# Dilated keys in a stage of their own: Strassen's seven block products, two projection units at a time, and rotations that exchange halves by transfers

## The chip, the cores and the metric

The kernel runs on one core of one Trainium2 chip. The metric is the device time of one execution in microseconds; lower is better. The kernel before takes 1445.66 us (median of 3 runs, 1445.48 to 1445.92).

Engines are named as the profile names them: PE is TensorE's matmul stream and PEld its weight loads, DVE is VectorE, ACT ScalarE, POOL GpSimd, SP the engine whose queue issues most transfers.

## What is computed

An encoder block on x of 1024 tokens x 1024 channels. `h = rms_norm(x)` is projected by `w_in` to the inputs of three parallel mixers and their gates. This case is about the first mixer, dilated window attention with 3 groups of 8 heads (head size 64), at windows and dilations (128, 1), (512, 4), (2048, 16):

```python
aq = rope(a_qkv[:, :, 0], pos)
ak = rope(a_qkv[:, :, 1], pos)
av = a_qkv[:, :, 2]
for gi, (window, dil) in enumerate(A_GROUPS):
    o_g, lse_g = dilated_window_attention(aq[:, :, hs], ak[:, :, hs], av[:, :, hs], window, dil)
oa = sum over the groups, weighted by softmax of their log-denominators

def rope(x, pos):                      # per head: x1, x2 are its halves of 32
    return concat([x1 * cos - x2 * sin, x1 * sin + x2 * cos])
```

The other mixers are global attention with axial rotary positions and attention into a fixed memory of 256 tokens. Each mixer is gated by SiLU, projected, merged by sigmoid gates and projected again; a normalised sum with x is the output.

## The kernel before, in words

All is computed in float32 precision by three float32r passes: each operand is split into a high part (ACT copy, L105) and a low part (DVE subtraction, L106), and each product is high x high + high x low + low x high. `h` (up to its row factors) stays in SBUF all the time as `hh` and `hl`, 8 tiles of 128 channels x 1024 tokens each.

A **unit** is 128 output channels of a projection: two halves of 512 tokens, 24 matmuls of 128x512 each (`dense`, L139 on; L143, L145 and L147 are its three passes), in two PSUM banks `d`. Each half is evacuated by the unit's own function. Units stand in `queue`; `prepare` loads and splits a unit's weights one unit ahead (buffers `wr`, two, and `wh`/`wl`, two each). PE's order is written out by hand: `weave` runs the dense matmuls of some units and a list of attention pieces in parallel, each piece having a declared cost, so that both progress in proportion. In some stages DVE, ACT, POOL and SP follow the written order too (`manual_schedule`); elsewhere the scheduler orders them.

The stages that matter, by time in the profile:

- The **value stage** (461.8 to 581.4 us, L836 to L1012, all engines in written order) makes the values of the three dilation groups. One group is made in the classical way (16 steps of 12 matmuls, `v_first`), then the other two together by Strassen's seven block products of 512 x 512 (`PRODUCTS`, L844; 28 steps of 12 matmuls). The operands S1 to S4 are sums of weight blocks (`sum_at`, on POOL, L902), T1 to T4 sums of token blocks, made earlier and kept in DRAM as `tsd`. `split_at` splits operands two steps ahead, `blocks_at` loads token blocks five steps ahead. `v_evac` combines products on DVE, `v_store` scales on ACT and stores to DRAM (`vdr`). Between the steps, `operand` rescales the global mixer's output (L942, L943) in eight pieces, one every 4 steps, through single buffers `vot`, `vgt`, `vrt`. The rotation tables `tab` are loaded and scaled here as well.
- The **dilated stage** (581.4 to 1007.9 us, L1018 to L1410) works on 12 items: 4 head pairs x 3 groups. An item needs its query and its key unit, rotated. `rope_half` (L1040) does it for half a unit: four 32-partition DVE multiplications with the sine that read the other half of the head from PSUM, one of 128 partitions with the cosine, and an addition on POOL (L1056), which also regroups tokens by residue class. Three units run before the first scores (`weave(3)`, L1387, written order), then two units beside each item's attention. The pieces of an item (`plan`, L1242): scores of four query tiles at a time (L1137), `soft` per tile (DVE minimum L1149, ACT exponential L1150), transposes of a tile two tiles later (L1167 or L1176, copied out by ACT, L1179, from one of two banks `tr`), and twice an item the products with the values (L1193, copied out by ACT, L1201). Values are loaded for each item between its two score blocks (L1081 on). After every third item the groups are combined (`combine`, L1297). In the last two items four gate units run in place of queries and keys.
- The **closing gate stage** (1007.9 to 1219.6 us) makes 22 gate units in 11 pairs by the same seven products, one product being 12 matmuls into one bank. Its token blocks T1 to T3 are loaded during the last item into buffers that are free by then.

Of the kernel before, what the change touches and what calls it, by code (L numbers as in the profile page):

```python
# [15 lines left out]
S = 1024  # L16
NT = 8
P = 128
# [32 lines left out]
def block(ctx: ExitStack, tc: tile.TileContext, x, xT, memT, cst, msk, bcst, tabA, gpost,  # L51
# [181 lines left out]
    vdr = dram.tile([3, 4, S, 128], F32, name="vdr")  # L233

# [410 lines left out]
    def first_values():  # L645

        hl_ = []
        for i in range(2):
            raw = wp.tile([P, 1024], F32, name="wr", bufs=WR)
            nc.sync.dma_start(raw.rearrange("p (k f) -> p k f", k=2), wv[VG[0], :, 2 * i:2 * i + 2])  # L650
# [186 lines left out]
    v_first = ready.pop(len(queue))  # L837
# [3 lines left out]
    tbp, tb = pool("tb")  # L841
    tab = [tb.tile([P, S], F32, name=f"tab{j}") for j in range(2)]
    vpp, vp = pool("vp")
    PRODUCTS = (("A11", "B11"), ("A12", "B21"), ("S2", "T2"), ("S3", "T3"), ("S4", "B22"), ("S1", "T1"), ("A22", "T4"))  # L844
# [7 lines left out]
    slots0 = [slot() for _ in range(4)]  # L852
    def rs():
        return vp.tile([P, 512], F32, name="vr", bufs=5)

    raw1 = vp.tile([P, 4, 512], F32, name="sum1")
    for i in range(2):
        nc.sync.dma_start(raw1[:, 2 * i:2 * i + 2], wv[VG[0], :, 4 + 2 * i:6 + 2 * i])
    VR = {}
    for nm, u, kh in (("A21", 1, 0), ("A11", 0, 0), ("A22", 1, 1), ("A12", 0, 1)):  # L860
        VR[nm] = vp.tile([P, 4, 512], F32, name=f"v{nm}")
        for i in range(2):
            nc.sync.dma_start(VR[nm][:, 2 * i:2 * i + 2], wv[VG[1 + u], :, 4 * kh + 2 * i:4 * kh + 2 * i + 2])
    VR.update(S1=raw1, S3=VR["A21"], S2=VR["A11"], S4=VR["A12"])
    vv = [vp.tile([P, 512], F32, name=f"vv{j}") for j in range(4)]
    vy = [vp.tile([P, 512], F32, name=f"vy{j}") for j in range(4)]
    SB, TB_ = {}, {}
# [13 lines left out]
    def split_at(i, k):  # L881
        an, bn = PRODUCTS[i]
# [25 lines left out]

    def v_out(u, t, j, ps_, z):
        r = rs()  # L910
# [21 lines left out]
    def operand(r, stage):  # L932
        k, t = r // 2, half[r % 2]
        if stage == 0:
            OT[r] = [vp.tile([P, 512], F32, name=x) for x in ("vot", "vgt", "vrt")]
# [17 lines left out]
    FIRST = 16  # L953
    steps_v = [(None, e, k) for e in range(2) for k in range(8)] + [(i, 0, k) for i in range(7) for k in range(4)]
    left = []
    for n, (i, e, k) in enumerate(steps_v):
        if k == 0:
            now = v_banks()
        for j in range(4):
            if i is None:  # L960
                t = slice(e * 512 + j * 128, e * 512 + j * 128 + 128)
                (bh, bl), w, end = (hh[k][:, t], hl[k][:, t]), v_first[k], 7
# [6 lines left out]
        if n + 2 < 8 and n + 2 >= 4:  # L969
            v_first.append(slots0[n - 2])  # L970
            split(*parts_of(v_first[-1]), raw1[:, n - 2])
        m = n + 2 - FIRST
        if 0 <= m < 28:
            split_at(*divmod(m, 4))
        for f in behind:
            f()
        m = n + 5 - FIRST
        if 0 <= m < 28:
# [8 lines left out]
        if n == FIRST + 10:  # L987
            for j in range(2):
                nc.sync.dma_start(tab[j], tabA[:, j])
        if n == FIRST + 17:  # L990
            V.tensor_tensor(tab[0], tab[0], rb, op=OP.mult)
            G.tensor_tensor(tab[1], tab[1], rb, op=OP.mult)
        if n == FIRST + 16:
            early[len(queue)] = lambda: [wp.tile([P, 1024], F32, name="wr", bufs=WR)]
            prepare(len(queue))
            nc.sync.dma_start(ready[len(queue)][0], wu[0])
        if n == FIRST + 25:
            raw = ready.pop(len(queue))[0]
            w = wslot(0), wslot(1)
            split(*w, raw)  # L1000
            ready[len(queue)] = tuple(z.rearrange("p (k f) -> p k f", k=8) for z in w)
        if k == end:
            for j in range(4):
                if i is None:
                    left.append(lambda b=now[j], T=4 * e + j: [lambda: v_store(rs(), VG[0], T, b)])
                else:
                    left.append(lambda i=i, j=j, b=now[j]: v_evac(i, j, b))
    for f in left:
        for g in f():
            g()  # L1010
    manual.__exit__(None, None, None)
    close(vpp)  # L1012
# [7 lines left out]
    with tc.tile_pool(name="aa", bufs=1, reuse_waits="tile") as aa:  # L1020
# [19 lines left out]
        def rope_half(o, half, p, scale, g):  # L1040

            t = slice(half * 512, half * 512 + 512)
            t1 = ab.tile([P, 512], F32, name="t1a", bufs=3)
            t2 = ab.tile([P, 512], F32, name="t2a", bufs=3)
            cos, sin = tab[0][:, t], tab[1][:, t]

            def mult(out, x, y):
                if scale is None:
                    return V.tensor_tensor(out, x, y, op=OP.mult)  # L1049
                return V.scalar_tensor_tensor(out, x, scale, y, op0=OP.mult, op1=OP.mult)  # L1050
# [5 lines left out]
            G.tensor_tensor(half_of(o, half, g), classes(t1, g), classes(t2, g), op=OP.add)  # L1056

        def add_a(p_, g):
            base = (p_ * 3 + g) * 2
# [803 lines left out]
```

## Time and profile before

| | |
|---|---|
| median of 3 runs | 1445.66 us |
| the profiled execution | 1445.34 us |
| span of its trace | 1443.5 us |
| PE, PEld busy | 1420.8, 1142.4 us |
| DVE, ACT, POOL busy | 979.8, 631.7, 499.7 us |
| transfers | 168.26 MB, mean 117 GB/s |
| TensorE clock granted | 0.999 |

The page splits the span by engine and gives the chain of work that ended last. A busy PE is not PE at its peak: a matmul of 128x512 is shown 389 ns long, while the next may start sooner, so what counts is the distance between starts. A row of the windows table holds, for each engine, its busy time in that stretch and the number of instructions.

### The profile page before, as it was taken

To read this page: it belongs to the slowest core of one execution; us is meant where nothing else is said; L and a number is where in the kernel's file an instruction comes from. 1 tells how busy PE (TensorE), PEld (TensorE's weight loads), DVE (VectorE), ACT (ScalarE), POOL (GpSimd) and SP (SyncE) were. 2 spreads that over 40 slices of the span, in tenths; PEclk is the share of its full clock that TensorE was granted. 3 is DMA by queue.
4 is the path that set the end of the run, shared out by engine and by line. 5 is a ranking of instruction groups with operands and counts; after the bars stand their busy time and mean duration, and the time that the engine had idled before them with its cause. 6 is when DMAs were issued, how large, how long until landed. Compare 5 with 4: busy or idle time off the path is not lost.

```text
span 1443.5 us, 20974 instructions
## 1 busy us (share of the span) xinstructions
PE 1420.8 (98%) x7628; PEld 1142.4 (79%) x7628; DVE 979.8 (68%) x1723; ACT 631.7 (44%) x1361; POOL 499.7 (35%) x382
## 2 busy tenths in 40 slices
PE   7999999999999999999999999999999999999998
PEld 7899986566666888888788888778887888888887
DVE  7765468776772267775697686864778778559643
ACT  6544355665654253244444534554443434223231
POOL 1415504666674421232233241321333331044322
PEclk9999999999999999999999999999999999999999
DMA  6332012232111775511132142343444453757122
GB/s 238 104 117 74 16 66 92 81 97 83 55 52 40 249 226 181 152 48 43 47 94 76 53 105 54 99 129 88 141 147 139 175 175 116 285 205 286 41 89 102
DMA packets 99448, 168.26 MB, mean 117 GB/s; under 512 B 21968, under 2 KB 51728, under 8 KB 99344
## 3 DMA queue, kind: packets, MB, share of 16 engines
q1 hardware_dynamic: 80192, 148.95, 32.1%
q10 hardware_dynamic: 19152, 17.96, 3.7%
q8 instruction: 60, 0.98, 0.3%
q14 instruction: 44, 0.36, 0.1%
HBM read 124.57 MB, written 42.30 MB: 116 GB/s over the span
## 4 chain that ended last, share of the span: by engine, by line
PE 76%; DVE 12%; ACT 4%; issue 4%; POOL 3%; DMA 1%; ACTq 0%; SPq 0%; POOLq 0%; DVEq 0%
PE sc L125 9%; PE s L125 8%; PE d L145 8%; PE d L143 8%; PE d L147 8%; PE s L967 6%; PE sc L1709 5%; PE ov L754 3%; PE tr L1193 2%; PE d L967 2%; PE s L738 2%; PE tr L720 2%; PE s L739 2%; PE d L535 2%; PE s L1137 2%
## 5 line engine op out<-in xcount | busy, mean ns | idle before, releaser
L143 PE MATMUL d<-hh,wh 128*128 128x512 f32 x672 | 270.2, 402 | 2.2 <-DVE fth L222 1.7
L145 PE MATMUL d<-hl,wh 128*128 128x512 f32 x672 | 268.0, 399 | 0.0
L147 PE MATMUL d<-hh,wl 128*128 128x512 f32 x672 | 267.9, 399 | 0.0
L105 ACT ACTIVATE wh<-wr 128x1024 fp32r<-128x1024 f32 (+1 forms) x79 | 72.2, 916 | 212.0 <-PE d L145 116.7
L143 PEld LDWEIGHTS d<-hh,wh 128*128 128x128 f32 x672 | 126.5, 188 | 32.6 <-issue 3.9
L145 PEld LDWEIGHTS d<-hl,wh 128*128 128x128 f32 x672 | 126.6, 188 | 29.9 <-issue 6.6
L745 POOL TENSOR_TENSOR bl<-bl,bp 128x512 f32<-128x512 f32 x96 | 131.4, 1369 | 53.7 <-ACT bp L741 48.2
L147 PEld LDWEIGHTS d<-hh,wl 128*128 128x128 f32 x672 | 126.5, 188 | 28.5 <-issue 4.5
L125 PE MATMUL sc<-hh,wh 128*128 128x512 f32 x384 | 118.5, 389 | 0.0
L1056 POOL TENSOR_TENSOR aq<-t1a,t2a 128x512 f32<-128x512 f32 x24 | 45.5, 1897 | 171.2 <-DVE t1a L1050 157.1
L1150 ACT ACTIVATE pra<-pra,sts 128x192 f32<-128x192 f32 (+2 forms) x192 | 84.2, 440 | 32.5 <-DVE sts L1149 32.4
L721 DVE TENSOR_REDUCE bn<-tr 128x1 f32<-128x512 f32 x128 | 86.0, 685 | 17.4 <-PE tr L720 16.1
L741 ACT ACTIVATE bp<-s 128x512 f32<-128x512 f32 x128 | 75.8, 595 | 46.7 <-PE s L739 45.8
L106 DVE TENSOR_TENSOR wl<-wr,wh 128x1024 fp32r<-128x1024 f32 x53 | 73.6, 1390 | 31.9 <-ACT wh L105 31.5
L1050 DVE SCALAR_TENSOR_TENSOR t2a<-d,tab 32x512 f32<-32x512 f32 x96 | 66.0, 687 | 38.3 <-PE d L147 36.7
L1056 POOL TENSOR_TENSOR ak<-t1a,t2a 128x512 f32<-128x512 f32 x24 | 55.1, 2294 | 103.8 <-DVE t1a L1049 103.8
L1049 DVE TENSOR_TENSOR t2a<-d,tab 32x512 f32<-32x512 f32 x96 | 66.0, 687 | 34.6 <-PE d L147 33.2
L125 PEld LDWEIGHTS sc<-hh,wh 128*128 128x128 f32 x384 | 72.1, 188 | 14.9
L1436 POOL TENSOR_TENSOR sf<-wr 128x512 f32<-128x512 f32 x22 | 31.0, 1427 | 146.2 <-DMA wr<-in_wu 60.5
L1640 POOL TENSOR_TENSOR acc<-acc,th 128x1024 f32<-128x1024 f32 x15 | 40.9, 2727 | 110.1 <-DVE th L1639 110.1
L125 PE MATMUL sc<-hl,wh 128*128 128x512 f32 x192 | 74.7, 389 | 0.0
L1149 DVE CUSTOM_DVE_ANT_0 pra<-s,mask 128x192 f32<-128x192 f32 (+2 forms) x192 | 55.9, 347 | 17.3 <-PE s L1137 15.5
(369 smaller groups left out, 3396.2 us busy)
## 6 DMA issues: line engine op xcount, KB each, us to landing
wr<-in_wu SPq DMA_DIRECT2D x64, 512.0 KB
th<-thd SPq DMA_DIRECT2D x24, 512.0 KB
thd<-rs ACTq DMA_DIRECT2D x44, 256.0 KB
g2d<-fth SPq DMA_DIRECT2D x24, 256.0 KB
vdr<-vr ACTq DMA_DIRECT2D x24, 256.0 KB
wgt<-wgd SPq DMA_DIRECT2D x24, 256.0 KB
ot<-od SPq DMA_DIRECT2D x12, 512.0 KB
wr<-in_wbr SPq DMA_DIRECT2D x24, 256.0 KB
```

The costliest lines, as they stand in the source:

```text
L105: A.activation(dst_h, src, AF.Copy)
L106: V.tensor_tensor(dst_l, src, dst_h.bitcast(F32), op=OP.subtract)
L125: PE.matmul(out_ps, a, b, start=i == 0, stop=i == n - 1)
L143: PE.matmul(dst, wh[:, k, :], hh[k][:, t], start=k == 0, stop=False)
L145: PE.matmul(dst, wh[:, k, :], hl[k][:, t], start=False, stop=False)
L147: PE.matmul(dst, wl[:, k, :], hh[k][:, t], start=False, stop=k == 7)
L721: fp["last"] = V.tensor_reduce(st[i]["n"][:, j, c:c + 1], s, axis=AX.X, op=OP.min)
L741: A.activation(pp, s, AF.Exp, scale=-1.0)
L745: G.tensor_tensor(lsum[i % 2], lsum[i % 2], pp, op=OP.add)
L967: PE.matmul(now[j], a, b, start=k == 0 and q == 0, stop=k == end and q == 2)
L1056: G.tensor_tensor(half_of(o, half, g), classes(t1, g), classes(t2, g), op=OP.add)
L1150: A.activation(src, src, AF.Exp, scale=-1.0, bias=bias, accum_out=sts[:, h, 1, T:T + 1])
```

## The change

- Strassen's value products come first in the value stage, the classical group second (16 steps, weights loaded and split as it goes). S1 and S2 are summed at steps 2 to 5, S3 at 7 to 10, S4 at 11 to 14, and `operand` runs every 3 steps.
- A **key stage** is new: the 12 key units in 6 pairs, each pair by the same seven products of 12 matmuls. The 16 token blocks T1 to T4 are loaded and split once (most of them during the classical value steps) and stay in SBUF for all six pairs. Sums of weights are made on POOL, products combined on DVE, keys stored in DRAM unrotated (`kd`).
- The dilated stage runs only the query unit beside each item (`weave(1)`; before the first scores `weave(2)`). A key is fetched back with a second copy whose 32-row quarters are exchanged by four transfers, and rotated by two DVE multiplications of 128x1024 in SBUF and two POOL subtractions, while the item two before it runs (fetched at its tile 0, rotated at its tile 5).
- A query half is multiplied by sine and cosine in two 128-partition DVE instructions; the sine product's quarters are exchanged by four SBUF to SBUF transfers before POOL's addition.
- Tables are loaded and scaled in the key stage. Some buffers change: `t1a`, `t2a` have 2 copies, the exchanged product `t3a` one, and the closing stage's token blocks use the key buffers `kraw`, `kswp`.

The diff, cut to its core:

```diff
+    kd = dram.tile([12, P, S], F32, name="kd")
...
-    steps_v = [(None, e, k) for e in range(2) for k in range(8)] + [(i, 0, k) for i in range(7) for k in range(4)]
+    CLASSIC = 28
+    steps_v = [(i, 0, k) for i in range(7) for k in range(4)] + [(None, e, k) for e in range(2) for k in range(8)]
...
-        for nm, s0 in (("S1", 7), ("S3", 11), ("S2", 17), ("S4", 21)):
+        for nm, s0 in (("S1", 2), ("S2", 2), ("S3", 7), ("S4", 11)):
...
-            r, at = divmod(n - 6 - (0, 2, 3)[stage], 4)
+            r, at = divmod(n - 6 - (0, 2, 3)[stage], 3)
...
+    def k_load(n, u):
+        KR[n, u] = wp.tile([P, 1024], F32, name="wr", bufs=WR)
+        nc.sync.dma_start(KR[n, u], wu[4 * n + 2 * u + 1])
...
+    def k_out(n, u, t, ps_, z):
+        r = kp.tile([P, 512], F32, name="kr", bufs=4)
+        V.tensor_tensor(r, ps_, z, op=OP.add)
+        return lambda: nc.scalar.dma_start(kd[2 * n + u, :, half[t]], r)
...
+    for n in range(6):
+        for i, (an, bn) in enumerate(PRODUCTS):
+            dst = pss1()
+            ah, al = [z.rearrange("p (k f) -> p k f", k=4) for z in BK[n, an]]
+            terms = []
+            for k in range(4):
+                bh, bl = k_tokens(bn, k)
+                terms += [(ah[:, k], bh), (ah[:, k], bl), (al[:, k], bh)]
+            passes(dst, terms)
...
-            for a in range(4):
-                i, j = slice(32 * a, 32 * a + 32), slice(32 * (a ^ 1), 32 * (a ^ 1) + 32)
-                mult(t2[i], p[j], sin[j])
-            fp["last"] = mult(t1, p, cos)
+        def swapped(dst, src):
+            for a in range(4):
+                nc.sync.dma_start(dst[32 * a:32 * a + 32], src[32 * (a ^ 1):32 * (a ^ 1) + 32])
+
+        def q_rope(o, half, p, g):
+            t = slice(half * 512, half * 512 + 512)
+            t1, t2, u = [(ab if j == 1 else aa).tile([P, 512], F32, name=f"t{j}a", bufs=2 if j < 3 else 1) for j in (1, 2, 3)]
+            V.scalar_tensor_tensor(u, p, -0.125, tab[1][:, t], op0=OP.mult, op1=OP.mult)
+            fp["last"] = V.scalar_tensor_tensor(t1, p, -0.125, tab[0][:, t], op0=OP.mult, op1=OP.mult)
+            swapped(t2, u)
             G.tensor_tensor(half_of(o, half, g), classes(t1, g), classes(t2, g), op=OP.add)
...
+        def k_fetch(p_, g):
+            KK[p_, g] = [ab.tile([P, S], F32, name=x) for x in ("kraw", "kswp")]
+            nc.sync.dma_start(KK[p_, g][0], kd[p_ * 3 + g])
+            swapped(KK[p_, g][1], kd[p_ * 3 + g])
+
+        def k_rope(p_, g):
+            kr, ks = KK.pop((p_, g))
+            V.tensor_tensor(kr, kr, tab[0], op=OP.mult)
+            V.tensor_tensor(ks, ks, tab[1], op=OP.mult)
+            ka = OPS.setdefault((p_, g), {})["k"] = ab.tile([P, S], F32, name="ak", bufs=2)
+            for x in range(2):
+                t = half[x]
+                G.tensor_tensor(half_of(ka, x, g), classes(kr[:, t], g), classes(ks[:, t], g), op=OP.subtract)
...
+                if it and it["ahead"] and T in (0, 5):
+                    out.append((lambda T=T: keys(it["ahead"], T), 0.0))
...
-        weave(3)
+        k_fetch(*seq[0])
+
+        def first_keys():
+            yield 300.0
+            k_rope(*seq[0])
+            k_fetch(*seq[1])
+            yield 400.0
+            k_rope(*seq[1])
+            yield 300.0
+
+        weave(2, first_keys(), 1000.0)
...
-            weave(len(GATES_A) - 1 if last else 2, run(pieces), sum(c for _, c in pieces), 1.0)
+            weave(len(GATES_A) - 1 if last else 1, run(pieces), sum(c for _, c in pieces), 1.0)
```

More of the change, by code (lines that the diff above doesn't have):

```diff
@@ new lines, in k_own, with k_block, k_tokens @@
+    def k_own(n):
+        h, l = wslot(0), wslot(1)
+        split(h, l, KR[n, 0])
+        for j in range(2):
+            BK[n, ("A11", "A12")[j]] = h[:, half[j]], l[:, half[j]]
+    def k_block(n, nm):
+        t = kp.tile([P, 1024], R, name="ch", bufs=5)
+        split(*parts_of(t), k_part(n, 3) if nm == "A22" else SF[int(nm[1]) - 1])
+        BK[n, nm] = parts_of(t)
+    def k_tokens(bn, k):
+        if bn[0] == "T":
+            return parts_of(KT[bn, k])
+        kk, t = k + 4 * (bn[1] == "2"), (lo, hi)[bn[2] == "2"]
+        return hh[kk][:, t], hl[kk][:, t]
@@ L983, in block @@
         for stage in (2, 1, 0):
-            r, at = divmod(n - 6 - (0, 2, 3)[stage], 4)
+            r, at = divmod(n - 6 - (0, 2, 3)[stage], 3)
             if at == 0 and 0 <= r < 8:
                 operand(r, stage)
[L987 to L1001, printed above, removed]
+        if n == CLASSIC + 4:
+            close(vbp)
+            tpp, tp = pool("tp", "right")
+            SF = [tp.tile([P, 512], F32, name=f"sf{j}") for j in range(4)]
+        m = n - CLASSIC - 4
+        if m >= 0:
+            for z in kt_all[2 * m:2 * m + 2] if m < 4 else kt_all[m + 4:m + 5]:
+                kt_load(*z)
+            for z in kt_all[2 * m - 6:2 * m - 4] if 3 <= m < 7 else kt_all[m + 1:m + 2] if 7 <= m < 11 else ():
+                kt_split(*z)
+            if m == 6:
+                k_load(0, 0)
+                k_load(0, 1)
+            elif m == 10:
+                k_own(0)
+            elif m == 11:
+                k_sum(0, 1)
+                k_sum(0, 2)
         if k == end:
@@ L1011, in block @@
+    for f in left.pop(0)():
+        f()
     manual.__exit__(None, None, None)
-    close(vpp)
+    close(kpp)
+    close(tpp)
     end_psum()
@@ L1259, in tokens, with keys @@
                     load_block("T1", (0, 1))
+            def keys(key, T):
+                if T == 0:
+                    k_fetch(*key)
+                else:
+                    with tc.issue_after(fp["last"].ins):
+                        k_rope(*key)
             def ready():
```

178 lines of the change are left out of this document (123 added, 55 removed).

## The prediction

> **What bounds the kernel now.** Read first the page's head, busy times and chain: is one engine always last?
>
> ```profile
> span 1443.5 us, 20974 instructions
> PE 1420.8 (98%) x7628; PEld 1142.4 (79%) x7628; DVE 979.8 (68%) x1723; ACT 631.7 (44%) x1361; POOL 499.7 (35%) x382
> PE 76%; DVE 12%; ACT 4%; issue 4%; POOL 3%; DMA 1%; ACTq 0%; SPq 0%; POOLq 0%; DVEq 0%
> ```
>
> PE is busy 98% and carries 76% of the chain. Busy alone proves little, since matmuls overlap in the pipeline; so read next the spacing of matmul starts, in the chain of waits in order of time (start, us, what), at the start and end of the value stage and later in the output projections:
>
> ```profile
> 461.82 23.13 PE s L967 x102
> ...
> 570.63 10.88 PE s L967 x48
> ...
> 1219.60 130.56 PE sc L125 x576
> ```
>
> 23.13/102, 10.88/48 and 130.56/576 all give 226.7 ns per 128x512 matmul. The value stage has 2 x 8 x 12 + 28 x 12 = 528 of them: 119.7 us. Now PE's timeline, the first matmul behind that stage and the first of the closing gate stage:
>
> ```profile
> 581.35 0.39 PE L143 MATMUL d<-hh,wh 128*128 128x512 f32 x1
> ...
> 1007.89 0.50 PE L125 MATMUL s<-hh,wh 128*128 128x512 f32 x1
> ```
>
> 461.82 to 581.35 is 119.5 us: the value stage has no gap at all. The dilated stage lasts 1007.89 - 581.35 = 426.5 us; its 28 projection units of 48 matmuls (24 queries and keys, 4 gates) make 1344 x 0.2267 = 304.7 us of that. The windows table, four stretches inside it (us; busy of PE, PEld, DVE, ACT, POOL; clock; DMA share; GB/s):
>
> ```profile
> 680.00:740.00 60.00, 59.91 (x389) 48.43 (x388) 42.13 (x107) 28.52 (x89) 16.20 (x8) 1.00 0.23 62
> 740.00:800.00 60.00, 59.68 (x405) 48.39 (x403) 46.27 (x109) 26.62 (x89) 18.04 (x11) 1.00 0.31 80
> 800.00:860.00 60.00, 59.57 (x404) 47.86 (x403) 50.10 (x114) 29.65 (x90) 21.36 (x10) 1.00 0.31 81
> 860.00:920.00 60.00, 59.91 (x393) 48.34 (x392) 38.93 (x107) 28.37 (x86) 14.48 (x8) 1.00 0.19 55
> ```
>
> PE never rests, at full clock. DVE is at 177.4/240 = 74%, ACT 47%, POOL 29%: near enough to matter if PE gets shorter. So matmuls taken away are time won, until an engine or a latency steps into the hole.
>
> **The change part by part.** *Keys leave the dilated stage:* 12 units x 48 = 576 matmuls, 576 x 0.2267 = **-130.6 us**. *The key stage:* 6 pairs x 7 products x 12 = 504 matmuls. Ungapped that is 114.3 us; the closing stage, with the same seven products for 11 pairs (924 matmuls), took 1219.60 - 1007.89 = 211.7 us, 229.1 ns each, with its starting waits in it. I take its rate: **+115.5 us** (114.3 to 120, the upper end being twice its loss again plus a late start). Beside 19 us of matmuls per pair, DVE has about 10 us (7 evacuations, one whole and five half splits at the prices below), so it hides.
>
> *The value stage* keeps its 528 matmuls but starts with Strassen, whose operands are needed earlier. Its start before, on SP, ACT, POOL and DVE:
>
> ```profile
> 467.37 0.84 SPq L858 DMA_DIRECT2D sum<-in_wv  x2
> 468.31 6.55 SPq L863 DMA_DIRECT2D vA<-in_wv  x8
> ```
>
> ```profile
> 471.13 2.39 ACT L105 ACTIVATE sl<-sum 128x512 fp32r<-128x512 f32 x4 [7.74 <-DMA sum<-in_wv]
> ```
>
> ```profile
> 479.99 5.03 POOL L902 TENSOR_TENSOR sum<-vA,vA 128x512 f32<-128x512 f32 x4 [21.49 <-DMA vA<-in_wv]
> ```
>
> ```profile
> 489.26 1.75 DVE L943 TENSOR_TENSOR vot<-vot,vrt 128x512 f32<-128x512 f32 x1 [2.46 <-DMA vrt<-rld]
> ```
>
> The first two loads become A12, wanted at the same point as before (four steps of 2.72 us, at 472.7), and the first split at 471.13 just makes it. S2 is wanted at step 8, 483.6; its pieces are loads 3 to 5 instead of 5 to 8, and POOL could begin near 475: in time. But DVE runs in written order, and the first rescaling of the global mixer (L942, L943) sits at step 8, waiting for its transfers until 489.26 and ending at 491.0; behind it now stand an evacuation and two splits (0.68 us each) for step 11, due at 491.7. They end at 493.1: **+1.5 us** (0 to 6, the latter if each of the eight rescalings, now every 3 steps, costs 0.75).
>
> *Start of the dilated stage.* Two units instead of three run before the first scores, and both keys are rotated in them, in written order. Nearest rows, a load's issue and the instruction that it releases:
>
> ```profile
> 464.26 0.33 SPq L826 DMA_DIRECT2D rl<-lbd  x1
> ```
>
> ```profile
> 466.36 0.55 DVE L827 RECIPROCAL rl<-rl 128x64 f32<-128x64 f32 x1 [2.62 <-DMA rl<-lbd]
> ```
>
> A small transfer takes 2.1 us. The first query half ends 24 matmuls in (5.4 us); one more 0.7 us multiplication, four issues (some 1.6), 2.1 of transfer and POOL's add bring 11.7; POOL then adds the first key (two adds), 16.3; only then may the second key's fetch overwrite the single buffer, and SP, in order, waits there with the next exchange behind it. Its five issues and 1 MB (512 KB landed 471.13 - 467.37 = 3.8 us behind its issue) reach about 22, its multiplications 24.5. Behind them on DVE waits the second query's first half, whose PSUM bank PE wants back at 96 x 0.2267 = 21.8 us. **+4 us** (0 to 8).
>
> *The items.* Values and scores blocks, and the small transposes (chain of waits):
>
> ```profile
> 660.25 1.90 PE tr L1193 x32
> 662.14 1.69 PE s L1137 x17
> ...
> 665.23 0.33 PE tr L1167 x3
> ...
> 755.88 1.90 PE tr L1193 x32
> ```
>
> 660.25 to 755.88 is three items: 31.9 us each, 21.8 of it 96 projection matmuls. Without the key unit 21.0 us remain. Does DVE fit? Groups by form in 617.7 to 950 us, then the page and by-form groups of the whole run:
>
> ```profile
> L1049 DVE TENSOR_TENSOR t2a<-d,tab 32x512 f32<-32x512 f32 x88 | 60.5, 687 | 31.7 <-PE d L147 30.4
> ...
> L106 DVE TENSOR_TENSOR wl<-wr,wh 128x1024 fp32r<-128x1024 f32 x22 | 28.6, 1300 | 0.3
> ...
> L1049 DVE TENSOR_TENSOR t1a<-d,tab 128x512 f32<-128x512 f32 x22 | 15.2, 691 | 0.6
> ```
>
> ```profile
> L106 DVE TENSOR_TENSOR hl<-raw,hh 128x1024 fp32r<-128x1024 f32 x4 | 13.7, 3415 | 0.0
> ...
> L281 DVE TENSOR_TENSOR acc<-acc,xk 128x1024 f32<-128x1024 f32 x7 | 8.5, 1220 | 0.3
> ```
>
> ```profile
> L1056 POOL TENSOR_TENSOR aq<-t1a,t2a 128x512 f32<-128x512 f32 x24 | 45.5, 1897 | 171.2 <-DVE t1a L1050 157.1
> ...
> L1056 POOL TENSOR_TENSOR ak<-t1a,t2a 128x512 f32<-128x512 f32 x24 | 55.1, 2294 | 103.8 <-DVE t1a L1049 103.8
> ```
>
> A 32-partition multiplication costs as much as a 128-partition one. DVE now spends 74% of 31.9 = 23.6 us per item; the key's ten (6.9), six of the query's ten (4.1) and a weight split (1.3) go, two 128x1024 multiplications from SBUF come. At L281's 1.22 us that leaves 13.8 us of 21.0 (66%); at 3.4 us, what the same shape took beside POOL, 18.1 (86%). I take the low end's neighbourhood, POOL being at 9.3 us of 21. ACT keeps 14 us (67%). So no engine overtakes PE on average, and the DVE time saved wins nothing by itself.
>
> What could hurt is latency. Behind a scores block, the rows of PE, DVE and ACT:
>
> ```profile
> 757.70 1.81 PE L1137 MATMUL s<-ak,aq 64*128 64x128 f32 x24
> 760.70 0.49 PE L1167 MATMUL tr<-cs,pra 128*128 128x128 f32 x3
> ...
> 763.69 0.49 PE L1167 MATMUL tr<-cs,pra 128*128 128x128 f32 x3
> ```
>
> ```profile
> 760.07 0.44 ACT L1150 ACTIVATE pra<-pra,sts 128x192 f32<-128x192 f32 x1
> ...
> 762.27 0.47 ACT L1179 ACTIVATE app<-tr 128x384 f32<-128x384 f32 x1
> ```
>
> The third transpose group starts 4.3 us behind the scores; 0.7 of that is transposes, and the other 3.6, projections, halve: it is wanted at 761.9. Its softmax is done at 760.5, fine. But it reuses one of two PSUM banks, which ACT's copy frees at 762.74, since six exponentials went ahead. That is up to 0.85 us of PE wait, at two such blocks per item: 1.7 us. The order on ACT is the scheduler's and can change, and DVE's queue is shorter, so gains are possible too. I take 0.4 us per item, **+5 us** (-4 to +20).
>
> Transfers: values loads must land between two values blocks, 15 us apart now, some 8 us then. The longest was issued at 722.25 and had moved by 726:
>
> ```profile
> 722.25 0.40 SPq L1090 DMA_DIRECT2D avs<-vdr  x1
> ```
>
> ```profile
> 725.00:726.00 1.00, 1.00 (x7) 0.78 (x7) 0.97 (x5) 1.00 (x6) 0.00 (x0) 1.00 0.36 108
> ```
>
> 3.8 us: hidden. SP gains 12 issues per item (1 for keys, 4 + 8 for exchanges, one weight load less): at 0.4 us 5 of 21 us, hidden while nothing urgent stands behind a wait.
>
> *Costed at nothing.* The 16 token blocks that the key stage keeps are loaded and split in the value stage's eight-step part, 16 x 0.69 = 11 us of DVE. That part's window before:
>
> ```profile
> 461.40:522.60 61.20, 61.20 (x271) 50.70 (x270) 23.80 (x28) 19.25 (x33) 22.89 (x16) 1.00 0.68 224
> ```
>
> DVE is 39% busy there, and hides them (uncovered: 11 us). The query's add on POOL now waits for its exchange, with key adds queued behind; who needs them are scores an item later, 20 us off. Stores of keys are 24 ACT issues of about 0.4 us, beside PE in a stage where ACT has little else.
>
> **Sum**, on the profiled execution's 1445.34 us (span 1443.5 and 1.8 around it; 0.3 under the median 1445.66): 1445.3 - 130.6 + 115.5 + 1.5 + 4 + 5 = 1440.7; on the median's footing **1441 us**.
>
> **The rivals.** *(1) PE alone counts:* no new waits, items lose some old ones: 1445.7 - 130.6 + 114.3 - 4 = 1425 to 1431. For it: the gapless value stage; against: softmax waits that the windows show already (0.1 to 0.4 us of PE idle in 60).
> *(2) Slower: the transposes wait for ACT.* Place: PE in front of the third transpose group behind each scores block, price 1.7 us x 12 = 20: 1436 + 20 = 1456. The sum without the items' term is 1436, so it decides from (1445.7 - 1436)/12 = 0.8 us per item. DVE multiplications stretched by POOL to 3.4 us would feed it, by late softmax inputs. The Trainium skill speaks for that: "SBUF - State Buffer", section on SBUF's two separate sides, says that a VectorE instruction with two SBUF inputs and a GpSimd instruction exclude each other for their whole length. The long rows above (3415 against 1220 ns) agree, though not what they waited for. By that rule every key rotation could cost an add's length more.
> *(3) Written order bites at the two starts,* at the upper ends 6 and 8 instead of 1.5 and 4: 1450. For it: DVE's wait until 489.26.
>
> **How the numbers follow.** Forecast 0.45 (1432 to 1442.7, faster), rival 1 0.10, rival 2 0.22, rival 3 0.08, between forecast and rivals, about unchanged, 0.15. 0.2% is 2.9 us, about what a measurement of this kernel can tell from no change: faster 0.55, within 0.15, slower 0.30. Range 1430 to 1457: what lies under it and over rival 2 is left out.
>
> **What would show it.** The key stage's seven-product pairs take 19.2 us each; items 21 to 21.5 us from values block to values block. PE waits for the small transposes' ACT copy, above 0.8 us per item, would prove rival 2; waits at the first matmuls of the third unit, the start term; DVE waiting for vrt with PE idle behind it, the value term. Items at 20 us prove rival 1. Wrong altogether: DVE over 90% in the items, or PE waiting for kraw or kswp.

## Result: 7% slower, and the profile after

| | before | after |
|---|---|---|
| median | 1445.57 us (1445.38 to 1445.92) | **1546.59 us** (1544.46 to 1548.59) |
| ratio | | 1.0698, 95% interval 1.068 to 1.0717 |
| profiled execution, span | 1445.34, 1443.5 us | 1544.46, 1542.7 us |
| TensorE clock granted | 0.999 | 0.971 |

The page of the changed kernel: head, busy times, chain by engine.

```profile
span 1542.7 us, 21224 instructions
PE 1431.0 (93%) x7556; PEld 1144.9 (74%) x7556; DVE 937.8 (61%) x1637; ACT 655.8 (43%) x1407; POOL 532.1 (34%) x406
PE 68%; DMA 9%; DVE 9%; ACT 5%; issue 4%; POOL 3%; SPq 2%; ACTq 0%; DVEq 0%; POOLq 0%
```

PE's busy time went *up* by 10 us although the change takes away 72 matmuls, its share of the span fell from 98 to 93%, and transfers, 1% of the chain before, now carry 9%. Where? The windows table, one row for each stage from PE's first matmul in it (columns as in the prediction):

```profile
462.00:597.60 135.60, 124.77 (x530) 100.78 (x529) 83.39 (x109) 53.58 (x90) 32.06 (x20) 0.97 0.70 225
597.60:713.80 116.20, 116.20 (x506) 94.57 (x505) 65.09 (x82) 30.71 (x49) 34.50 (x22) 1.00 0.35 122
713.80:1105.80 392.00, 312.99 (x2166) 250.74 (x2164) 178.53 (x529) 176.73 (x550) 108.57 (x55) 0.90 0.42 116
```

The key stage is gapless: 116.2 us. The value stage takes 135.6 instead of 119.5. The dilated stage takes 392.0; the prediction's terms give 426.5 - 130.6 + 4 + 5 = 304.9. Of the miss of 104 us, 87 are there and 15 in the value stage. No engine but PE is over 46% busy in the dilated stage, so this is waiting, and a PE at a granted clock of 0.90. PE's waits from 455 to 1110 us (total, times, longest):

```profile
PE d L143 <- DVE t1a L1183: 46.8, 7, 9.1
PE s L1279 <- POOL aq L1185: 22.6, 2, 14.5
PE s L1029 <- DVE sl L106: 8.0, 4, 3.7
PE tr L1348 <- ACT app L1321: 6.9, 5, 3.7
```

The first, seven times, is a PSUM bank that DVE has not evacuated. Why DVE is late can be read at the start of the dilated stage. PE, then DVE, POOL and SP:

```profile
724.46 0.39 PE L147 MATMUL d<-hh,wl 128*128 128x512 f32 x1
729.17 0.76 PE L143 MATMUL d<-hh,wh 128*128 128x512 f32 x1 [4.33 <-DVE t1a L1183]
...
751.72 0.76 PE L143 MATMUL d<-hh,wh 128*128 128x512 f32 x1 [9.07 <-DVE t1a L1183]
```

```profile
734.10 0.69 DVE L1182 SCALAR_TENSOR_TENSOR t3a<-d,tab 128x512 f32<-128x512 f32 x1 [2.81 <-DMA t2a<-t3a]
...
742.59 1.23 DVE L1207 TENSOR_TENSOR kraw<-kraw,tab 128x1024 f32<-128x1024 f32 x1 [7.19 <-DMA kraw<-kd]
743.73 1.22 DVE L106 TENSOR_TENSOR wl<-wr,wh 128x1024 fp32r<-128x1024 f32 x1
...
750.28 0.69 DVE L1182 SCALAR_TENSOR_TENSOR t3a<-d,tab 128x512 f32<-128x512 f32 x1 [4.20 <-DMA t2a<-t3a]
```

```profile
735.40 2.55 POOL L1212 TENSOR_TENSOR ak<-kraw,kswp 128x512 f32<-128x512 f32 x2
750.32 1.27 POOL L1185 TENSOR_TENSOR aq<-t1a,t2a 128x512 f32<-128x512 f32 x1 [12.37 <-DMA t2a<-t3a]
```

```profile
737.98 0.33 SPq L1202 DMA_DIRECT2D kraw<-kd  x1
738.35 1.82 SPq L1176 DMA_DIRECT2D kswp<-kd  x4
744.97 0.35 SPq L114 DMA_DIRECT2D wr<-in_wu  x1
745.37 6.14 SPq L1176 DMA_DIRECT2D t2a<-t3a  x5
```

Read it backwards. PE waits until 751.72 for DVE, which itself waits for `t3a` until 750.28; `t3a` is still the source of an exchange. Its data stood there since 734.8 (734.10 + 0.69), but SP issued that exchange only at 745.37: SP was waiting until 737.98 for POOL's key adds, issued the keys, waited for a weight buffer until 744.97, and only then came to the exchange. That weight buffer was free only when DVE's split at 743.7 was done, behind the key multiplication that was waiting for the keys. Four engines wait in a circle through one queue in order.

### The profile page after: what moved, and what is told of

Read it like the earlier page. It is cut to its first block, busy times and chain, and to the rows that moved or that the text cites. A ratio compares the mean times of both kernels' runs of the same rounds, so it can differ in the third digit from the quotient of the medians.

```text
span 1542.7 us, 21224 instructions
## 1 busy us (share of the span) xinstructions
PE 1431.0 (93%) x7556; PEld 1144.9 (74%) x7556; DVE 937.8 (61%) x1637; ACT 655.8 (43%) x1407; POOL 532.1 (34%) x406
## 4 chain that ended last, share of the span: by engine, by line
PE 68%; DMA 9%; DVE 9%; ACT 5%; issue 4%; POOL 3%; SPq 2%; ACTq 0%; DVEq 0%; POOLq 0%
PE s L125 15%; PE sc L125 8%; PE d L143 6%; PE d L145 5%; PE d L147 5%; PE sc L1871 4%; PE ov L755 3%; PE s L1029 3%; DMA t2a<-t3a 2%; PE tr L1335 2%; PE s L1279 2%; PE s L739 2%; PE tr L721 2%; PE s L740 2%; DMA wr<-in_wu 2%
## 5 line engine op out<-in xcount | busy, mean ns | idle before, releaser
L143 PE MATMUL d<-hh,wh 128*128 128x512 f32 x480 | 200.8, 418 | 48.6 <-DVE t1a L1183 46.8
L147 PE MATMUL d<-hh,wl 128*128 128x512 f32 x480 | 198.4, 413 | 0.0
L145 PE MATMUL d<-hl,wh 128*128 128x512 f32 x480 | 196.6, 410 | 0.0
L143 PEld LDWEIGHTS d<-hh,wh 128*128 128x128 f32 x480 | 93.7, 195 | 72.3 <-DVE t1a L1183 35.3
L105 ACT ACTIVATE wh<-wr 128x1024 fp32r<-128x1024 f32 (+1 forms) x75 | 67.2, 898 | 170.7 <-PE sc L125 76.0
L145 PEld LDWEIGHTS d<-hl,wh 128*128 128x128 f32 x480 | 93.9, 196 | 21.8 <-issue 6.3
L147 PEld LDWEIGHTS d<-hh,wl 128*128 128x128 f32 x480 | 93.0, 194 | 22.6 <-issue 5.0
L106 DVE TENSOR_TENSOR ch<-sf,ch 128x512 fp32r<-128x512 f32 x68 | 58.4, 860 | 42.1 <-ACT ch L105 42.1
L1598 POOL TENSOR_TENSOR sf<-wr 128x512 f32<-128x512 f32 x22 | 31.2, 1437 | 142.5 <-DMA wr<-in_wu 62.1
L125 PE MATMUL s<-hh,ch 128*128 128x512 f32 x224 | 74.1, 392 | 1.5 <-ACT ch L105 1.5
L978 POOL TENSOR_TENSOR sf<-wr 128x512 f32<-128x512 f32 x12 | 20.9, 1745 | 145.3 <-DMA wr<-in_wu 97.9
```

What stands on the lines that cost most here:

```text
L105: A.activation(dst_h, src, AF.Copy)
L106: V.tensor_tensor(dst_l, src, dst_h.bitcast(F32), op=OP.subtract)
L125: PE.matmul(out_ps, a, b, start=i == 0, stop=i == n - 1)
L143: PE.matmul(dst, wh[:, k, :], hh[k][:, t], start=k == 0, stop=False)
L145: PE.matmul(dst, wh[:, k, :], hl[k][:, t], start=False, stop=False)
L147: PE.matmul(dst, wl[:, k, :], hh[k][:, t], start=False, stop=k == 7)
```

## Experiments

Stage lengths are taken as in the table above (V value, K key, D dilated stage). K was 116.2 or 116.3 in every run.

| run | median us | ratio to before, 95% | V | D |
|---|---|---|---|---|
| changed kernel | 1546.6 | 1.068 to 1.072 | 135.6 | 392.0 |
| e1_q_old | 1514.9 | 1.046 to 1.049 | 135.8 | 359.5 |
| e2_swap_act | 1495.6 | 1.033 to 1.036 | 137.6 | 338.8 |
| e3_late_fetch | 1556.3 | 1.074 to 1.078 | 136.6 | 402.6 |
| e4_cadence4 | 1546.1 | 1.067 to 1.071 | 132.8 | 392.1 |
| e5_no_exchange | 1498.3 | 1.033 to 1.037 | 137.3 | 343.5 |
| e6_two_buffers | 1544.9 | 1.067 to 1.070 | 138.4 | 388.0 |
| e7_act_two_buffers | 1505.1 | 1.039 to 1.042 | 138.4 | 349.1 |
| e8_all_four | 1480.0 | 1.020 to 1.026 | 123.5 | 332.5 |
| e9_swap_first | 1570.5 | 1.084 to 1.088 | 139.1 | 415.3 |
| e10_one_buffer | 1478.4 | 1.021 to 1.025 | 123.3 | 336.8 |
| e11_stats_later | 1477.0 | 1.020 to 1.024 | 123.1 | 334.0 |
| e12_stats_and_copies | 1475.4 | 1.019 to 1.022 | 123.1 | 335.2 |
| e13_cover | 1565.5 | 1.081 to 1.084 | 123.3 | 424.6 |
| e14_bare | 1441.5 | 0.995 to 0.998 | 123.2 | 300.9 |
| e15_pool_queue | 1498.1 | 1.034 to 1.038 | 123.4 | 352.0 |
| e16_no_key_rotation | 1456.1 | 1.005 to 1.009 | 123.0 | 316.2 |
| e17_keys_alone | 1476.1 | 1.019 to 1.023 | 122.9 | 335.1 |
| e18_no_key_adds | 1446.6 | 0.999 to 1.001 | 122.9 | 305.2 |

Ten of these runs (e1, e3, e5, e7, e9, e12, e14, e15, e16, e18) ended outside every range of time written down for them; e14, e16 and e18 missed the nearest by some 3 us or less.

**First set: what holds the exchange?** By theory A it is the exchange's place on SP's queue, by theory B the ring DVE - exchange - POOL itself; by theory C the loss is not the exchange but rival 2 of the prediction.

e1, queries rotated as before:

```diff
-            V.scalar_tensor_tensor(u, p, -0.125, tab[1][:, t], op0=OP.mult, op1=OP.mult)
+            for a in range(4):
+                i, j = slice(32 * a, 32 * a + 32), slice(32 * (a ^ 1), 32 * (a ^ 1) + 32)
+                V.scalar_tensor_tensor(t2[i], p[j], -0.125, tab[1][j, t], op0=OP.mult, op1=OP.mult)
...
-            swapped(t2, u)
```

> The changed kernel, with queries rotated as before (four 32-partition multiplications from PSUM, no exchange, t3a gone); keys still come from DRAM with their exchange. Theory A (the 88 us that the dilated stage took over its forecast come from the queries' exchanges, which stand behind everything else on SP's queue) and theory B (they come from the ring DVE - exchange - POOL add itself, however early it is issued): the stage falls from 393 to 315-335 us, the time to 1465-1490. Theory C (softmax, ACT and DVE latencies, rival 2 of the prediction; DVE's work goes up by 4 us an item here): 1530 or more.

D fell by 32.5 us, half of what A and B asked for. PE's waits at L143 fell from 46.8 to 13.8 us, but its waits of the statistics' transposes for ACT rose from 6.9 to 30.8: with DVE loaded again (247.8 us busy in the stage instead of 178.5), C appears.

e2, the exchange on another queue:

```diff
-            swapped(t2, u)
+            for a in range(4):
+                nc.scalar.dma_start(t2[32 * a:32 * a + 32], u[32 * (a ^ 1):32 * (a ^ 1) + 32])
```

> The changed kernel, with the queries' exchanges alone issued from ACT's queue instead of SP's. Theory A: no exchange stands behind k_fetch, weights, values and combining loads any more, so POOL's wait of 141 us for t2a<-t3a falls under 60 and the time to 1480-1505. Theory B: the ring stays as long, 1530-1545. Theory C, and the 96 issues of some 0.5 us now on ACT: 1545-1580.

Beside one store of keys at its start, ACT's queue carries no other transfer in this stage. D fell by 53 us and the time to 1495.6, within A's range; the detail was wrong, POOL's wait for the exchange fell only from 141 to 127 us, and B's ring is not gone.

e3, the fetch of keys at another step:

```diff
-                if it and it["ahead"] and T in (0, 5):
+                if it and it["ahead"] and T in (3, 6):
```

> The changed kernel, with keys fetched at step 3 of an item instead of step 0 and rotated at step 6 instead of 5, so that the fetch finds the keys' adds done. SP's 60 us of waits at L1202 for POOL's ak go. Theory A, if that wait is the main holder of the queue: 1500-1525. If the loads ahead on the queue hold it instead: 1535-1550. Theory B: within 5 us of 1546.

```profile
SPq L1202 <- POOL ak L1212: 59.9, 11, 7.7
```

10 us *slower*, outside all three ranges. But the edit did not do what it was for: SP still waits 59.9 us for POOL's key adds (60.1 before). So A in its narrow form, that the key fetch's wait is the holder, was not tested; the run shows only that this other order does not help.

e4, the value stage:

```diff
-            r, at = divmod(n - 6 - (0, 2, 3)[stage], 3)
+            r, at = divmod(n - 1 - (0, 2, 3)[stage], 4)
```

> The changed kernel, with the rescaling rounds of the value stage every fourth step from step 1 on, instead of every third from step 6. If the rounds (8.3-8.7 us each from store to load against 8.16 us of three steps) make the 16 us that the value stage lost, it falls from 135.8 to 120-125 us and the time to 1532-1537. If splits on DVE, stretched beside POOL's sums, make them: value stage 133 or more, time within 4 us of 1546.

V is 132.8, just under the second range, and the time is that of the changed kernel. The changed kernel's gaps on PE's timeline in this stage, then those here:

```profile
497.58 4.28 PE L1029 MATMUL s<-sl 128*128 128x512 f32 x11 [3.71 <-DVE sl L106]
...
550.65 0.50 PE L1029 MATMUL d<-wh,hh 128*128 128x512 f32 x1 [2.73 <-DVE vr L909]
...
563.83 1.22 PE L1029 MATMUL s<-sl,hh 128*128 128x512 f32 x2 [3.56 <-DVE sl L106]
```

```profile
488.52 1.22 PE L1029 MATMUL s<-wh,hh 128*128 128x512 f32 x2 [9.26 <-DVE wh L106]
```

The late gaps are gone and one of 9.26 us is new: DVE stands, in written order, at an early rescaling whose operand arrives late behind the value weights. So the rounds do cost, but not by their cadence.

**Second set: price and buffers.** e5 leaves the exchange out (the sine product goes straight into `t2a`, which has two buffers), e6 gives `t3a` two buffers and takes one of the two of the gates' `fth` for it, e7 is e2 and e6 together.

```diff
-            swapped(t2, u)
-            G.tensor_tensor(half_of(o, half, g), classes(t1, g), classes(t2, g), op=OP.add)
+            G.tensor_tensor(half_of(o, half, g), classes(t1, g), classes(u, g), op=OP.add)
```

```diff
-name=f"t{j}a", bufs=2 if j < 3 else 1) for j in (1, 2, 3)]
+name=f"t{j}a", bufs=2) for j in (1, 2, 3)]
```

> The changed kernel without the queries' exchange: POOL adds the two products as they are, so queries are left unrotated across the halves (that part of the computation is left out); DVE's work is that of the changed kernel. The price of the exchange as a whole. If it makes all that the dilated stage lost: stage 305-318 us, time 1458-1472. If the waits of transposes for ACT (30.8 us with queries rotated on DVE, 14.9 us with the exchange on ACT's queue) come with the shorter cover of PE and not with the exchange: stage 325-340, time 1478-1493.

> The changed kernel with two buffers for t3a, paid for with one buffer for fth in this stage; the exchange stays on SP's queue. If the single buffer is what turns a late exchange into PE's waits (DVE stands at t3a for 43 us, and does not free the PSUM bank): waits at L143 fall from 46.8 us to under 20, time 1495-1520. If lateness itself is what counts (POOL's add, then scores, wait as long): 1530-1547.

> The exchange on ACT's queue and two buffers for t3a. DVE's 38.9 us of waits at t3a go. If they feed the transposes' waits (late softmax inputs): 1475-1487. If not: 1491-1498.

e5's D of 343.5 is no better than e2's 338.8. So an exchange on ACT's queue costs, in this kernel, no more than none: its price of some 50 us is its place on SP's queue. It is not all the loss: without any exchange D is still 39 us over the forecast's 304.9. e6's waits:

```profile
PE s L1279 <- POOL aq L1185: 49.8, 4, 15.4
PE tr L1348 <- ACT app L1321: 17.4, 7, 3.6
PE d L143 <- DVE t1a L1183: 9.0, 2, 5.0
```

As hoped, L143 falls from 46.8 to 9.0, and the same time comes back at the scores, which wait for the queries: the buffer was where lateness showed, not its cause. With the exchange on ACT's queue (e7) the second buffer, with one `fth` less, even costs 10 us, outside both ranges; that did not repeat (e10 below, one buffer again, takes 1478.4 against e8's 1480.0).

e8 adds two things to e7: an earlier request for weights with the second key's rotation moved into item 0, and the rescaling in the key stage, staged in the tables' buffers, with the tables loaded later:

```diff
+        prepare(done[0])
+        prepare(done[0] + 1)
         k_fetch(*seq[0])
...
+            for stage in (2, 1, 0):
+                r, at = divmod(7 * n + i - 1 - (0, 2, 3)[stage], 4)
```

> As the kernel before in this list (exchange on ACT's queue, two buffers), with the weights of the second dilated unit asked for ahead of the first keys, the second keys rotated in the first item, and the rescaling rounds moved from the value stage into the key stage, every fourth product. Value stage: 119-123 us instead of 136 if the rounds are its loss, 130 or more if the splits are. Key stage 116-119. Start of the dilated stage: both waits at L143 (4.3 and 9.1 us in the changed kernel) under 2 us. Time 1448-1466; over 1475 if value stage or start keep their losses.

```profile
462.20:585.70 123.50, 121.50 (x530) 98.66 (x529) 72.60 (x93) 53.41 (x90) 31.61 (x20) 1.00 0.55 179
585.70:701.90 116.20, 116.20 (x506) 94.59 (x505) 74.59 (x99) 31.62 (x49) 35.03 (x22) 1.00 0.57 191
```

The value stage is at 123.5 and the key stage not 0.1 us longer: the rounds cost 12 of the 16 us, and are free where DMA and DVE have room. Of the other 4, 2.0 are PE's waits for DVE's splits (`sl`, `wl`) in e8's trace. The waits at L143 are gone, but the total, 1480, is over the expected range: D is still 332.5.

**Third set: the queue's order, and rival 2.** e9:

```diff
-            swapped(t2, u)
+            with tc.high_priority(offset=400):
+                swapped(t2, u)
```

> The changed kernel, with the queries' four exchange issues given precedence in SP's written order: still SP's queue, still one t3a, but each group of four stands together, ahead of weights, keys, values and combining loads that are not yet due. If the place in SP's order is the price of the exchange: as with ACT's queue, stage 335-350 us, time 1492-1512. If bulk transfers that are already under way on the same queue hold the small ones: 1525-1547.

The slowest of all. PE's waits:

```profile
PE tr L1319 <- ACT og L1344: 59.0, 2, 30.1
PE tr L1349 <- ACT app L1322: 16.3, 6, 5.9
PE tr L1336 <- DMA avs<-vdr: 14.4, 1, 14.4
```

The waits at L143 are down to 9.5, but now values come 14.4 us late, and twice PE waits some 30 us for ACT's `og`, which waits for the combining of groups, whose weights come late on the same queue (DVE waits 42.4 us for `wgt`). With e3: neither of two other orders on SP did better than the one given. Its list has waits on four engines, and whatever stands first holds up the rest.

e10 is e8 with one `t3a` and two `fth`. e11 moves the statistics' transpose, e12 also puts ACT's copy `app` forward:

```diff
-                if T == 2 and pre:
+                if T == 3 and pre:
                     out += [(lambda: None, 300.0), pre["stats"]]
```

```diff
-                A.activation(pp[:, :k], tp[:, :k], AF.Copy)
+                with tc.high_priority(offset=400):
+                    A.activation(pp[:, :k], tp[:, :k], AF.Copy)
```

> The exchange on ACT's queue, the new start and the rescaling in the key stage, but one buffer for t3a and two for fth as in the changed kernel (two t3a buffers gave 10 us more on ACT's queue). 1464-1474; over 1476 if that difference does not repeat.

> The same with the statistics' transpose (PE, L1349 in the last list) emitted at step 3 of the next item instead of step 2. It waited 1.0-2.9 us per item for ACT's app copy, which stood behind six exponentials. If those waits are the price of rival 2: they fall from 15 us to under 6, time 1452-1462. If they only move to the next transposes: within 4 us of the kernel before it in this call.

> The same as the one before, and ACT's copies out of the transposes' PSUM banks (app) given precedence over exponentials in its order. Under rival 2, PE waits for ACT in the stage fall under 6 us in all and the time to 1445-1457. If late softmax inputs follow (exponentials later, transposes of the next tile wait for pra): 1458-1470.

e11 lands on its second branch: waits at the statistics fall from 16.4 to 1.1 us, and those of the next transposes (L1310) rise from 4.7 to 15.4. e12 does not help either: 1475.4, over both of its ranges.

**Fourth set: what feeds these waits?** Three candidates: (a) items too short to cover them, (b) the load of the rotation on DVE and POOL, (c) the exchange's issues on ACT. All three runs start from e10. e13 gives items their second unit back, unread; e14 is e5's edit and the keys read as they are; e15 has `nc.gpsimd` in place of e2's `nc.scalar`.

```diff
+            if (p_, g) not in seq[:2]:
+                add_unit(wu[(p_ * 3 + g) * 2 + 1], lambda half, p: None)
```

```diff
-            V.tensor_tensor(kr, kr, tab[0], op=OP.mult)
-            V.tensor_tensor(ks, ks, tab[1], op=OP.mult)
...
-                G.tensor_tensor(half_of(ka, x, g), classes(kr[:, t], g), classes(ks[:, t], g), op=OP.subtract)
+            nc.sync.dma_start(ka, kd[p_ * 3 + g])
```

> The kernel with the exchange on ACT's queue, the new start and the rescaling in the key stage (1478), and in items 1 to 10 the key's projection again, as work that nobody reads: 10 units of 48 matmuls, 109 us at 227 ns, with their weights' loads and splits. (a) cover: PE's waits for ACT in the stage fall from 30 us to under 8, and the stage takes 337 + 109 - 20 to 30 = 416-426 us, the time 1557-1568. (b) or (c): waits stay at 25 or more, stage 440 or more, time 1582 or more.

> The new start and the rescaling in the key stage, without any exchange and without the keys' rotation: the queries' halves are added unexchanged and keys are read from DRAM as they are (both rotations are left out of the computation). DVE loses 2 x 1.2-2.6 us and POOL two adds per item. (b) rotation's load: PE's waits for ACT under 8 us, stage 305-315, time 1444-1455. (a) cover: waits 18 us or more, stage 322-335, time 1462-1476.

> As the 1478 us kernel, with the queries' exchanges issued from POOL's queue instead of ACT's. (c) the issues on ACT: waits for ACT under 15 us, 1460-1470. (a) or (b): 1474-1490, POOL's adds being held behind the issues.

```profile
701.70:1126.30 424.60, 410.78 (x2645) 331.59 (x2643) 210.72 (x539) 185.18 (x559) 108.33 (x55) 0.98 0.43 121
```

```profile
702.40:1003.30 300.90, 294.63 (x2165) 235.03 (x2164) 146.56 (x505) 171.41 (x549) 70.21 (x31) 1.00 0.39 111
```

Both (a) and (b) take the waits away: PE waits for ACT 3.5 us in e13's stage and 6.0 in e14's. In e13 109 us more of matmuls lengthen D by only 88, in e14 D is under the forecast's 304.9. e15 cannot decide (c): the 96 issues put 47.8 us on POOL, beside whose adds the last set finds the loss, and D rises to 352. But e17 below has no exchange and so no such issues, and keeps the loss: (c) falls by that run. So the loss needs a short item *and* the rotation's load. The last set asks which part of that load: e16 is e10 with e14's edit of the keys, e17 is e10 with e5's edit of the queries, e18 is e10 without POOL's two key adds:

```diff
-            V.tensor_tensor(kr, kr, tab[0], op=OP.mult)
+            V.tensor_tensor(ka, kr, tab[0], op=OP.mult)
             V.tensor_tensor(ks, ks, tab[1], op=OP.mult)
...
-                G.tensor_tensor(half_of(ka, x, g), classes(kr[:, t], g), classes(ks[:, t], g), op=OP.subtract)
```

> The 1478 us kernel (exchange on ACT's queue, new start, rescaling in the key stage), with keys read from DRAM as they are, unrotated (that part of the computation is left out); the queries' exchange stays. If the keys' rotation is the load that the short items can't take: waits for ACT under 10 us, stage 302-312, time 1443-1453. If it is the exchange: stage 322 or more, 1463-1475.

> The new start and the rescaling in the key stage, with the keys' rotation whole and the queries' exchange left out (queries unrotated across halves). If the exchange is the load: 1443-1453. If the keys' rotation is: 1463-1476.

> The 1478 us kernel without POOL's two key adds per item: DVE's two multiplications stay, the first writes the keys (rotation incomplete: that part is left out). If POOL's adds (4 us per item, queries' adds queued behind them, DVE's two-input instructions stretched beside them) are the load: 1448-1460. If DVE's multiplications and the transfers are: 1468-1480.

e18 loses 24 POOL adds of 2.0 us and 31.6 us of D (336.8 to 305.2), while all DVE multiplications and transfers stay; e17, without any exchange, keeps the loss (335.1). e16 leaves out more than e18, the adds and also the key's multiplications and exchange, and yet gains less, 20.6 us (D 316.2, between its two ranges). DVE's groups by form from 702 to 1035 us, in e10, in e18 and in e16:

```profile
L106 DVE TENSOR_TENSOR wl<-wr,wh 128x1024 fp32r<-128x1024 f32 x16 | 27.1, 1694 | 15.8 <-ACT wh L105 15.8
...
L1182 DVE SCALAR_TENSOR_TENSOR t3a<-d,tab 128x512 f32<-128x512 f32 x24 | 16.5, 687 | 65.7 <-DMA t2a<-t3a 32.4 <-PE d L147 23.2 <-PE s L1280 8.8
```

```profile
L106 DVE TENSOR_TENSOR wl<-wr,wh 128x1024 fp32r<-128x1024 f32 x17 | 21.4, 1259 | 27.5 <-ACT wh L105 25.6 <-PE tr L1333 1.8
...
L1182 DVE SCALAR_TENSOR_TENSOR t3a<-d,tab 128x512 f32<-128x512 f32 x24 | 16.5, 688 | 29.2 <-DMA t2a<-t3a 18.2 <-PE d L147 9.7 <-DMA kswp<-kd 1.1
```

```profile
L106 DVE TENSOR_TENSOR wl<-wr,wh 128x1024 fp32r<-128x1024 f32 x17 | 29.8, 1754 | 54.6 <-ACT wh L105 54.6
...
L1182 DVE SCALAR_TENSOR_TENSOR t3a<-d,tab 128x512 f32<-128x512 f32 x24 | 16.5, 686 | 40.9 <-DMA t2a<-t3a 27.7 <-PE d L147 10.2 <-DMA wr<-in_wu 3.1
```

Two links to DVE are seen in e18: the weights' splits, with two inputs in SBUF, are shorter (16 x 0.435 = 7 us), and DVE waits 14 us less for exchanges, whose consumer, the query's add, queues behind key adds. Neither carries e16's gain: its splits are as long as e10's (1754 and 1694 ns), and DVE's wait for exchanges is only 5 us shorter. One stall of e17 shows a whole chain (POOL; DVE; ACT; PE):

```profile
807.89 4.13 POOL L1212 TENSOR_TENSOR ak<-kraw,kswp 128x512 f32<-128x512 f32 x2 [13.79 <-DVE kswp L1208]
812.80 2.04 POOL L1185 TENSOR_TENSOR aq<-t1a,t2a 128x512 f32<-128x512 f32 x1 [0.78 <-DVE ceg L1472]
```

```profile
808.83 1.17 DVE L1469 TENSOR_TENSOR cmn<-cpt 128x16 f32<-128x16 f32 x1
...
810.52 1.53 DVE L1470 TENSOR_TENSOR cmn<-cmn,cpt 128x16 f32<-128x16 f32 x1
...
813.08 1.82 DVE L1475 TENSOR_TENSOR cdn<-ceg,cpt 128x48 f32<-128x48 f32 x1 [0.31 <-ACT ceg L1473]
...
816.97 1.22 DVE L106 TENSOR_TENSOR wl<-wr,wh 128x1024 fp32r<-128x1024 f32 x1
818.10 0.35 DVE L1291 CUSTOM_DVE_ANT_0 pra<-s,mask 128x192 f32<-128x192 f32 x1
```

```profile
818.56 0.46 ACT L1292 ACTIVATE pra<-pra,sts 128x192 f32<-128x192 f32 x1 [3.59 <-DVE sts L1291]
...
821.20 0.58 ACT L1321 ACTIVATE app<-tr 128x512 f32<-128x512 f32 x1
```

```profile
821.83 0.28 PE L1348 MATMUL tr<-cs,sts 128*32 128x128 f32 x1 [3.21 <-ACT app L1321]
```

Two operations on 16 elements, L1469 and L1470, take 1.17 and 1.53 us beside POOL's two key adds (one of the same size, L1477, takes 0.18); the second ends at 812.05, the key adds at 812.02. The 48-element product starts at 813.08 and ends at 814.90, with POOL's query add (814.84). The scores are done by 816.0, but DVE still has 2.3 us of other work; the softmax starts at 818.10; ACT has six exponentials ahead of the copy that frees PE's bank. Here key adds and a query add hold DVE in turn; that the same happens at the other stalls was not traced. Without the adds SP also no longer waits for them before it fetches a key again (62.0 us in e10). DVE's waits for what SP loads do not show a gain from this: those for keys fall from 11.3 to 5.5 us, those for combining weights rise from 0 to 20.5. Leaving instructions out also lets the scheduler order the rest anew. That the loss goes from the short items when the key adds are left out is shown; how e18's gain divides among shorter DVE instructions, POOL's order, SP's queue and the new order stays open, and e16 says that some 11 us can depend on it.

No version here that computes everything beats the kernel before; e14, which leaves both rotations out, is 0.3% under it. Adding keys on DVE instead of POOL was not tried.

## Why the prediction was wrong, step by step

- **Keys leave, -130.6: right as a count.** PE has 2166 instructions in the stage instead of 2742, 576 fewer. That e18's D of 305.2 meets the forecast's 304.9 is partly luck: it leaves the key adds out, and its start and queue are others.
- **Key stage, +115.5: right** (116.2).
- **Value stage, +1.5 (0 to 6): wrong**, +16. The step that failed is the bound "0.75 for each of the eight rescalings": it allowed for no wait for their transfers in a stretch where DMA is 70% busy (DVE waits there 11.5 us for `vgt` and 3.2 for `vrt`). e8 puts 12 us on them.
- **Start, +4 (0 to 8): too small.** PE's two waits alone are 13.4 us. I had named the mechanism but not that SP's next exchange also stands behind a weight buffer. What it cost alone stays open: from e2 to e10 its waits at L143 fall by 7.7 us and D only by 2, while a new wait of 5.9 us for the first softmax appears; from e7 to e8 they fall by 9.6 and D by 17.
- **SP's issues, costed at nothing "while nothing urgent stands behind a wait": the main failure**, some 50 us. The condition was stated and not checked: SP's longest waits in the changed kernel's dilated stage are these,

```profile
SPq L1202 <- POOL ak L1212: 60.1, 11, 7.3
SPq L1176 <- DVE t3a L1182: 27.9, 7, 6.7
SPq L223 <- DVE fth L222: 23.6, 6, 6.8
```

and behind a wait of the first line, at the start of the stage as read above, stands what DVE needs to free PE's bank; the others were not followed one by one. The exchanges' move to ACT's queue (e2) gave 51 us back. That the first line's wait alone holds them was not tested (e3).
- **"Needed an item later, 20 us off": wrong.** The add's *result* is needed late, but its *inputs* are buffers of DVE, and those are needed at the next half unit. Twice the result came too late as well: the scores wait 22.6 us for `aq`.
- **Items, +5; rival 2 at 20: right in mechanism, chosen too low, and named at another transpose.** e10's waits of transposes for `app` and `og` are 24 us, 2.0 us an item (1.7 forecast). The feed is POOL beside DVE, but not at the instructions named there. The Trainium skill, "SBUF — State Buffer", section "SBUF: two separate sides", says that a VectorE instruction with two SBUF inputs and a GpSimd instruction that reads SBUF exclude each other. The 48-element product above agrees (1.82 us; L1480, of the same size, takes 0.21). The price taken for the key multiplications, "the low end's neighbourhood", was right: 1.24 and 1.22 us in e10, 1.92 and 1.22 in e17, not 3.4. Longer are other instructions, those of the combining and the weights' splits (1694 ns in e10, 1300 before), which the sum left at their old prices.

The slower side was priced from one mechanism at 20 us; two of them, and a lower clock, came together.

## What to carry to other kernels

A transfer moved into the loop between two engines should not stand on a queue whose other issues wait for several engines; count not its issues but the waits ahead of it in the list, and what its source buffer holds up. Another queue is not better as such: here ACT's was (1478.4 us), POOL's was not (1498.1). Work taken off the busiest engine is also cover taken from every latency beside it: here Strassen's step saves (130.6 - 116.2)/12 = 1.2 us an item, and by e13 the shorter item let some 2 us of waits through ((109 - 88)/10). Move periodic work with operands from DRAM to where transfers have room.

## What the runs showed of the hardware

A stall can be paid twice. The windows right behind the two waits above (clock is the third column from the end):

```profile
729.17:734.28 5.11, 5.11 (x12) 4.00 (x13) 2.30 (x3) 0.00 (x0) 0.14 (x1) 0.52 0.47 150
751.72:755.00 3.28, 3.28 (x8) 2.38 (x8) 0.00 (x0) 0.00 (x0) 3.28 (x2) 0.57 0.08 20
```

Twelve matmuls take 5.11 us, 426 ns each instead of 227, though PE is "busy" all the while: about 2.4 us lost behind a wait of 4.33. Over the dilated stage PE is busy 313.0 us in the changed kernel at clock 0.90 and 294.2 in e18 at 1.00, for the same 2166 instructions: that is where PE's extra busy time comes from. The Trainium skill, "TensorE: Matmul & The Clock Gate", Part 1, tells of half rate after at least one idle window of about 3.4 us. The rate agrees. The length of a wait alone does not decide, though: behind e17's 3.21 us above starts stay 0.23 us apart, and behind a wait of 2.58 us in e8 (PE, at 825.06) they were 0.43 us apart.
